# Activation parts side by side, buffers 96 bytes on, and three orders of matmuls in the FFN input

## The chip, the cores and the metric

The kernel runs on one core of a Trainium2 chip. The metric is the device time of one execution in microseconds; less is better. Each kernel is executed several times, and one further execution is taken with the hardware profiler. Distances of two matmuls are given in nanoseconds, from start to start.

## What is computed

A decoder trunk of two layers over 256 positions of width 2048, in float32. Every sub-layer takes an RMS norm of the stream, modulates it by shift, scale and gate, which come from a conditioning vector, and adds its output to the stream. Layer 0 mixes positions by a gated recurrence and by attention with forget gates, layer 1 by gated linear attention. Both layers end with the SwiGLU FFN of width 5632, which is the part that the change touches most:

```python
def swiglu(h, w_in, w_out):
    a, u = jnp.split(h @ w_in, 2, axis=-1)
    return (jax.nn.silu(a) * u) @ w_out
...
        h = modulate(rms_norm(x, norm_ffn_gain[layer]), sh2, sc2)
        x = x + g2[:, None, :] * swiglu(h, ffn_w_in[layer], ffn_w_out[layer])
```

## The kernel before

**Split operands.** Matmuls run on float32r operands, which the engine takes in one pass at less than full precision. Each operand is therefore split into a high part (the value rounded) and a low part (the rest), and a product is hi·hi + hi·lo + lo·hi, summed in PSUM. Weights arrive from DRAM in tiles of 128 x 2048 floats (raw), and for every half of such a tile ACT writes hi (line 166) and DVE lo (line 168). Activations are kept in tiles of eight buffers called h: four blocks of 128 features, each for 256 positions, in both parts. Such a tile is [128, 2, 4, 256] before: all four blocks of the high part first, then all four of the low part. These tiles have the names hT_s, hT_f, hT_n (normed inputs) and ct_m, ct_f (mixer and FFN outputs).

**Two kinds of product.** An ordinary product (lines 192 to 194) has the activations as stationary operand, 128 positions at a time, and 512 columns of weights as moving operand; three matmuls for each block and each half of the positions. One with 16 blocks has 96 matmuls. There are 38 such products (4 acc_A, 8 acc_B, 8 acc_O, 12 acc_C, 2 acc_F, and the start's, acc_s, which amount to 4), and the FFN output, acc_G, has 22 blocks for each of 4 column tiles in each layer. A turned product (lines 204 and 205) is used for the FFN input. There the weights are stationary, and the activations move:

```python
                nc.tensor.matmul(o, hi[:, cs], both, start=(kt == 0), stop=False, skip_group_check=True)
                nc.tensor.matmul(o[:, :T], lo[:, cs], both[:, 0], start=False, stop=(kt == KT - 1), skip_group_check=True)
```

The operand `both` is the high and the low part of one block, 2 x 256 columns, read as two runs that lie 4 KiB apart. So the first of the two matmuls has 512 columns and writes hi·hi into the first and hi·lo into the second half of a PSUM bank; the second has 256 columns and adds lo·hi to the first half. The document calls the two a pair. Every matmul has a weight load of its own, also where two in a row have the same stationary operand.

**FFN.** The 5632 columns are 22 chunks of 256 gate and 256 value columns. Chunk 0 is an ordinary product, chunks 1 to 21 are turned, each in two halves of 32 pairs (16 blocks x 2 column tiles). After a half, `done` copies the second half of the bank (ACT, line 1158), adds the first half (DVE, line 1159), applies silu, multiplies and splits the result into a ct_f tile. The chunks form four groups, (0 to 5), (6 to 11), (12 to 17) and (18 to 21); the FFN output of a group (acc_G, four column tiles) is computed one chunk after the group's last, so it stands after chunks 6, 12, 18 and 21.

**Order.** `drive()` goes through the pieces of all products in one order, keeps weight splits three pieces ahead and loads up to six further, and puts the steps of the recurrences between them. Among these are narrow products (line 290, 128 stationary by 256 moving columns) and the decay exponents ex (line 470), which have 512 moving columns out of the constant lvl.

**Where buffers lie.** Pools are laid out one behind the other. In the built program, silu_c and cols lie at 16512 and 24704 bytes of each partition; ident, lvl, tri, lmask, cmask and st follow from 25792 on and start at multiples of 64. The raw tiles start at 56992, hi at 81568, lo at 97952, h at 114336; all of these, and the buffers behind them, start 32 bytes past a multiple of 64 (160 past a multiple of 256 for raw, hi, lo and h).

Of the kernel before, what the change touches and what calls it, by code (L numbers as in the profile page):

```python
# [7 lines left out]
F32 = mybir.dt.float32  # L8
F32R = mybir.dt.float32r
I32 = mybir.dt.int32  # L10
AF = mybir.ActivationFunctionType
ALU = mybir.AluOpType
# [3 lines left out]
P = 128  # L16
T = 256
D = 2048
KT = D // P
# [3 lines left out]
LEVELS = (64, 32, 16, 8, 4, 2, 1)  # L23
FFN_GROUPS = ((0, 6), (6, 12), (12, 18), (18, 22))
LOOKAHEAD = 2
RAWS = 3
HIS = 4
FIRST = 4
# [19 lines left out]
NCOLS = 270  # L48
# [17 lines left out]
def build(tc, ctx, a, out):  # L66
    nc = tc.nc
    const = ctx.enter_context(tc.tile_pool(name="const", bufs=1))
    small = ctx.enter_context(tc.tile_pool(name="small", bufs=2))
    rawp = ctx.enter_context(tc.tile_pool(name="rawp", bufs=RAWS))  # L70
    piecep = ctx.enter_context(tc.tile_pool(name="piecep", bufs=HIS))
    hpool = ctx.enter_context(tc.tile_pool(name="hpool", bufs=8))
# [3 lines left out]
    def ps_mix(name):  # L76
        return env["pm"].tile([P, 512], F32, tag="pm", name=name)

    def h_tile(name):
        return hpool.tile([P, 2, 4, T], F32R, tag="h", name=name)  # L80


    silu_c = const.tile([P, D], F32, name="silu_c")
    cols = const.tile([P, NCOLS], F32, name="cols")
    ident = const.tile([P, P], F32, name="ident")
    lvl = const.tile([P, 9 * P], F32R, name="lvl")
    tri = const.tile([P, 2 * P], F32R, name="tri")
# [52 lines left out]

    def add(name, w, act, done, before=None, rate=0.0, first=False, last=False, turned=False):
        p = Product(name, w, act, done, before, rate)
        p.first, p.last, p.turned = first, last, turned
        pieces.extend((p, k) for k in range(2 * len(w)))

    urgent = []
# [49 lines left out]
    def multiply_turned(p, k, hi, lo):  # L196

        for kk in range(4):
            kt = k * 4 + kk
            both = p.act(kt)  # L200
            for c in range(2):
                cs = slice(kk * 256 + c * P, kk * 256 + (c + 1) * P)
                o = p.ps[:, c]
                nc.tensor.matmul(o, hi[:, cs], both, start=(kt == 0), stop=False, skip_group_check=True)  # L204
                nc.tensor.matmul(o[:, :T], lo[:, cs], both[:, 0], start=False, stop=(kt == KT - 1), skip_group_check=True)  # L205

    def run_jobs(n):
        while jobs and n > 0:
# [26 lines left out]
    def drive():  # L235
        i = 0
        while i < len(pieces):
# [7 lines left out]
            run_jobs(quota())  # L245
            for m in range(i, i + max(n, LOOKAHEAD + 1)):
                split(m)
            for m in range(i + LOOKAHEAD + 1, min(i + LOOKAHEAD + 7, len(pieces))):
                load(m)
# [19 lines left out]
    def act_of(tiles):  # L269
        def act(kt, t=None):  # L270
            tl = tiles(kt // 4) if callable(tiles) else tiles[kt // 4]
            if t is None:
                return tl[:, :, kt % 4, :]
            sl = t if isinstance(t, slice) else slice(t * P, (t + 1) * P)
            return tl[:, 0, kt % 4, sl], tl[:, 1, kt % 4, sl]
        return act

    def narrow_product(pool, act, w, n, name):
# [68 lines left out]
    def norm_tile(t):  # L347

        acol, bcol, hT, name = env["norm"]
        pool = env["pool"]  # L350
        r = rstd_of(env["ss"], t, f"{name}{t}")
        diag = pool.tile([P, P], F32, tag="diag", name=f"diag_{name}{t}", bufs=1)
        env["diag"] = nc.vector.tensor_scalar(diag, ident, r, None, ALU.mult).ins
        for nb in range(4):
            ps = ps_mix(f"xT_{name}_{nb}_{t}")
            tm = pool.tile([P, 512], F32, tag="hm", name=f"hm_{name}_{nb}_{t}", bufs=2)
            for kk in range(4):
                sl = slice(kk * P, (kk + 1) * P)
                nc.tensor.matmul(ps[:, sl], env["x"][nb][:, t, sl], diag, start=True, stop=True)
            for kk in range(4):  # L360
                kt = nb * 4 + kk
                sl = slice(kk * P, (kk + 1) * P)
                if kk < 2:
                    nc.vector.tensor_scalar(tm[:, sl], ps[:, sl], acol[:, kt:kt + 1], bcol[:, kt:kt + 1], ALU.mult, ALU.add)
                else:
                    nc.scalar.activation(tm[:, sl], ps[:, sl], AF.Identity, bias=bcol[:, kt:kt + 1], scale=acol[:, kt:kt + 1])
            hv = hT[nb][:, 0, :, t * P:(t + 1) * P]
            lv = hT[nb][:, 1, :, t * P:(t + 1) * P]
            src = tm.rearrange("p (k t) -> p k t", k=4)
            nc.scalar.copy(out=hv, in_=src)  # L370
            nc.vector.tensor_tensor(lv, src, hv, ALU.subtract)  # L371
# [9 lines left out]
    def split_columns(src, gains, key, n):  # L381
        c, k0 = ct_pair(key, n)
        if gains is None:
            hv = c[:, 0, k0:k0 + 2].rearrange("p k t -> p (k t)")
            lv = c[:, 1, k0:k0 + 2].rearrange("p k t -> p (k t)")
            nc.scalar.copy(out=hv, in_=src)
            nc.vector.tensor_tensor(lv, src, hv, ALU.subtract)
        else:
            for k in range(2):
                s = src[:, k * T:(k + 1) * T]  # L390
                nc.scalar.activation(c[:, 0, k0 + k], s, AF.Copy, scale=gains[k])
                nc.vector.scalar_tensor_tensor(c[:, 1, k0 + k], s, gains[k], c[:, 0, k0 + k], ALU.mult, ALU.subtract)

    lines = {}

# [555 lines left out]
    def start():  # L951
# [13 lines left out]
        hT, raw_w, raw_m = [], {}, {}  # L965
# [25 lines left out]
        def operand(kt):  # L991
            if kt % 4 == 0:
                hT.append(h_tile(f"hT_s{kt // 4}"))
            h = hT[-1]
            k = slice(kt, kt + 1)
            tm = pool.tile([P, T], F32, tag="tm", name=f"tm_s{kt}")
            nc.scalar.activation(tm, xT[:, kt, :], AF.Identity, bias=modc[0, 0][:, k], scale=acol[:, k])
            nc.scalar.copy(out=h[:, 0, kt % 4], in_=tm)
            nc.vector.tensor_tensor(h[:, 1, kt % 4], tm, h[:, 0, kt % 4], ALU.subtract)

        fetch_columns(0)
        fetch_columns(1)
# [1 line left out]
        with tc.tile_pool(name="ps_t", bufs=4, space=PSUM) as pt:  # L1004
            env["pm"] = pt
            for nb in range(4):
                ps = ps_mix(f"c_{nb}")
                sl = slice(nb * 512, (nb + 1) * 512)
# [13 lines left out]
            for nb in range(4):  # L1022
# [5 lines left out]
                for half in range(2):  # L1028
                    ps = ps_mix(f"xT_{nb}_{half}")
# [4 lines left out]
                    k0 = nb * 4 + half * 2  # L1034
# [11 lines left out]
        for kt in range(KT):  # L1046
# [8 lines left out]
            for n in (1, 3, 0, 2):  # L1055
                hi, lo = ws[n // 2]
                sl = slice((n % 2) * 512, (n % 2 + 1) * 512)
                for t in range(2):
                    a_hi, a_lo = act(kt, t)
                    o = acc[n][t]  # L1060
# [93 lines left out]
    def done_ffn_turned(l, i, half):  # L1154

        def done(ps):
            s = env["pool"].tile([P, 2, T], F32, tag="fs", name=f"fs{l}_{i}_{half}")
            nc.scalar.copy(out=s, in_=ps[:, :, T:])
            nc.vector.tensor_tensor(s, s, ps[:, :, :T], ALU.add)
            if i == FFN_GROUPS[-1][1] - 1 and half == 1:  # L1160
                silu_then_exp_ln(s[:, 0], s[:, 0])
            else:
                nc.scalar.activation(s[:, 0], s[:, 0], AF.Silu)
            nc.vector.tensor_tensor(s[:, 0], s[:, 0], s[:, 1], ALU.mult)
            gi = group_of(i)
            c, k0 = ct_pair(f"f{l}{gi}", i - FFN_GROUPS[gi][0])
            nc.scalar.copy(out=c[:, 0, k0 + half], in_=s[:, 0])
            nc.vector.tensor_tensor(c[:, 1, k0 + half], s[:, 0], c[:, 0, k0 + half], ALU.subtract)
        return done

    def done_ffn(l, i):
# [50 lines left out]
    def quads(w):  # L1222
        return [w[qd] for qd in range(4)]

    def add_ffn(l, rate):
        w1, wt, w2 = a["ffn_w_in"], a["ffn_w_turned"], a["ffn_w_out"]
        n = 0
        for gi, (b, e) in enumerate(FFN_GROUPS):
            while n < min(e + 1, FFN_GROUPS[-1][1]):
                before = {0: lambda: begin_ffn(l), 4: lambda: begin_row(l)}.get(n)  # L1230
                if n == 0:
                    add(f"F{l}_{n}", quads(w1[l]), now_act, done_ffn(l, n), before, rate, True)
                else:
                    for half in range(2):
                        m = 2 * n + half - 2
                        add(f"F{l}_{n}_{half}", [wt[l, m, qd] for qd in range(2)], now_act, done_ffn_turned(l, n, half),
                            before if half == 0 else None, rate, turned=True)
                n += 1
            for nb in range(4):
                add(f"G{l}_{gi}_{nb}", [w2[l, b // 2 + qd, nb] for qd in range((e - b) // 2)], ct_act(f"f{l}{gi}"),  # L1240
                    done_ffn_out(l, gi, nb), rate=rate, last=gi == len(FFN_GROUPS) - 1 and nb == 3)
# [32 lines left out]
    for u in range(4):  # L1274
        for half in range(2):
            before = (lambda: job(fox_gates(), TICKS["fox_gates"])) if (u, half) == (0, 0) else None
# [119 lines left out]
```

## Time and profile before

| | |
|---|---|
| median of 3 runs | 2531.12 us (2529.35 to 2532.55) |
| profiled execution | 2535.65 us |
| its span, first to last instruction | 2533.9 us |
| PE matmul busy | 2469.4 us, 12492 matmuls |
| DVE busy | 1825.2 us |
| ACT busy | 1211.2 us |
| mean granted TensorE clock | 0.996 of 2.4 GHz |

The profile lists each matmul from its start to its modelled end, and successive matmuls overlap. So the busy time of a group says little of its cost; the distance between two starts does, or the number of them in a stretch of known length.

### The profile page before, as it was taken

What the parts mean: (1) busy time and instruction counts of PE and PEld (TensorE: products, weight loads), DVE (VectorE), ACT (ScalarE), POOL (GpSimd) and SP (SyncE); (2) the same over time, 40 slices, a digit from 0 to 9 for tenths busy, and PEclk for the clock granted to TensorE, in tenths of its full rate; (3) what the DMA queues carried; (4) which work ended last, traced back from release to release, by engine and by line L of the source; (5) the groups of instructions that cost most, each with busy time, mean ns of one, the idle gap of its engine ahead of it and who ended that gap; (6) DMA issues with size and microseconds to landing.
All of it is one profiled execution on the core that took longest, in us unless ns stands there. A gap on an engine that the chain in (4) does not pass through costs nothing.

```text
span 2533.9 us, 31800 instructions
## 1 busy us (share of the span) xinstructions
PE 2469.4 (97%) x12492; PEld 2078.0 (82%) x12492; DVE 1825.2 (72%) x2143; ACT 1211.2 (48%) x1768; POOL 89.4 (4%) x174
## 2 busy tenths in 40 slices
PE   5799999999999999999999999999999999999999
PEld 4678887887888888888888888888888888888887
DVE  6977887877788877777777777776686555555555
ACT  4365555545444444444445545554544344344443
POOL 0000000000000000000000000000000000000000
PEclk9999999999999999999999999999999999999999
DMA  9964767885798877777776566667476555555554
GB/s 382 421 262 150 279 255 284 345 314 208 281 358 344 313 275 292 283 272 292 285 274 226 205 243 235 244 254 272 172 299 244 199 183 184 199 183 185 197 183 150
DMA packets 93865, 647.69 MB, mean 256 GB/s; under 512 B 10418, under 2 KB 10994, under 8 KB 16402
## 3 DMA queue, kind: packets, MB, share of 16 engines
q1 hardware_dynamic: 70290, 476.59, 50.4%
q0 software_dynamic: 23424, 169.07, 17.6%
q8 instruction: 98, 1.61, 0.2%
q14 instruction: 53, 0.43, 0.0%
HBM read 641.39 MB, written 4.23 MB: 255 GB/s over the span
## 4 chain that ended last, share of the span: by engine, by line
PE 92%; DVE 6%; ACT 1%; issue 0%; DMA 0%; SPq 0%; ACTq 0%; DVEq 0%
PE acc_F L204 25%; PE acc_F L205 13%; PE acc_G L192 6%; PE acc_G L194 6%; PE acc_G L193 6%; PE acc_C L194 3%; PE acc_C L192 3%; PE acc_C L193 3%; DVE mod_s L108 3%; PE acc_B L192 2%; PE acc_B L194 2%; PE acc_B L193 2%; PE acc_O L192 2%; PE acc_O L193 2%; PE acc_O L194 2%; DVE lo_s L168 1%
## 5 line engine op out<-in xcount | busy, mean ns | idle before, releaser
L204 PE MATMUL acc_F<-hT_f,hi 128*128 128x512 f32 x2688 | 948.1, 398 | 0.0
L205 PE MATMUL acc_F<-hT_f,lo 128*128 128x256 f32 x2688 | 753.9, 280 | 0.0
L168 DVE TENSOR_TENSOR lo<-raw_F,hi 128x1024 fp32r<-128x1024 f32 x352 | 430.0, 1224 | 292.3 <-ACT hi L166 292.0
L166 ACT CAST hi<-raw_F 128x1024 fp32r<-128x1024 f32 x352 | 369.8, 1051 | 498.4 <-PE acc_F L204 281.0
L204 PEld LDWEIGHTS acc_F<-hT_f,hi 128*128 128x128 f32 x2688 | 504.9, 188 | 124.6
L205 PEld LDWEIGHTS acc_F<-hT_f,lo 128*128 128x128 f32 x2688 | 507.4, 189 | 0.6
L108 DVE SCALAR_TENSOR_TENSOR mod<-mod,silu_c 128x2048 f32<-128x2048 f32 x160 | 365.4, 2285 | 1.2 <-DMA mod<-in_mod_w_dram 1.2
L166 ACT CAST hi<-raw_G 128x1024 fp32r<-128x1024 f32 x176 | 185.3, 1054 | 273.2 <-PE acc_G L194 206.7
L168 DVE TENSOR_TENSOR lo<-raw_G,hi 128x1024 fp32r<-128x1024 f32 x176 | 214.3, 1223 | 133.4 <-ACT hi L166 133.3
L192 PE MATMUL acc_G<-hi,ct_f 128*128 128x512 f32 x704 | 273.9, 389 | 1.6 <-DVE res_G L419 1.6
L193 PE MATMUL acc_G<-lo,ct_f 128*128 128x512 f32 x704 | 273.9, 389 | 0.0
L194 PE MATMUL acc_G<-hi,ct_f 128*128 128x512 f32 x704 | 273.7, 389 | 0.0
L168 DVE TENSOR_TENSOR lo<-raw_C,hi 128x1024 fp32r<-128x1024 f32 x96 | 116.7, 1222 | 58.8 <-ACT hi L166 58.4
L192 PEld LDWEIGHTS acc_G<-hi,ct_f 128*128 128x128 f32 x704 | 132.2, 188 | 30.0 <-DVE res_G L419 2.4
L192 PE MATMUL acc_C<-hi,hT_n 128*128 128x512 f32 x384 | 154.3, 402 | 0.9 <-ACT hT_n L370 0.9
L194 PEld LDWEIGHTS acc_G<-hi,ct_f 128*128 128x128 f32 x704 | 132.1, 188 | 27.5
L193 PEld LDWEIGHTS acc_G<-lo,ct_f 128*128 128x128 f32 x704 | 132.2, 188 | 27.1
L194 PE MATMUL acc_C<-hi,hT_n 128*128 128x512 f32 x384 | 150.5, 392 | 0.7 <-DVE hT_n L371 0.7
L193 PE MATMUL acc_C<-lo,hT_n 128*128 128x512 f32 x384 | 150.9, 393 | 0.0
L166 ACT CAST hi<-raw_C 128x1024 fp32r<-128x1024 f32 x96 | 100.7, 1052 | 95.9 <-PE acc_C L194 89.5
L103 POOL DMA_DIRECT2D mod<-in_mod_w_dram x160 | 84.7, 530 | 1683.2 <-DVE mod L108 1542.2
L166 ACT CAST hi<-raw_O 128x1024 fp32r<-128x1024 f32 x64 | 67.4, 1054 | 80.9 <-PE acc_O L194 72.1
(345 smaller groups left out, 3485.8 us busy)
## 6 DMA issues: line engine op xcount, KB each, us to landing
raw_F<-in_ffn_w_turned_dram SPq DMA_DIRECT2D x168, 1024.0 KB, 4.8
mod<-in_mod_w_dram POOLq DMA_DIRECT2D x160, 1024.0 KB, 5.1
raw_G<-in_ffn_w_out_dram SPq DMA_DIRECT2D x88, 1024.0 KB, 4.8
raw_C<-in_gla_w_in_dram SPq DMA_DIRECT2D x48, 1024.0 KB, 5.7
mod_s<-in_mod_w_dram SPq DMA_DIRECT2D x32, 1024.0 KB, 10.8
raw_B<-in_ab_w_in_dram SPq DMA_DIRECT2D x32, 1024.0 KB, 5.6
raw_s<-in_start_w_dram SPq DMA_DIRECT2D x16, 1024.0 KB, 9.4
raw_A<-in_ab_w_in_dram SPq DMA_DIRECT2D x16, 1024.0 KB, 4.8
```

The lines of the kernel that those rows point to most:

```text
L103: nc.gpsimd.dma_start(out=tile, in_=a["mod_w"][l, part * KT + j])
L108: nc.vector.scalar_tensor_tensor(tile, tile, 1.0, silu_c, ALU.mult, ALU.mult, accum_out=modc[l, part][:, j:j + 1])
L166: nc.scalar.copy(out=hi, in_=w)
L168: env["lo"] = nc.vector.tensor_tensor(lo, w, hi, ALU.subtract)
L192: nc.tensor.matmul(o, a_hi, w_hi, start=(kt == 0), stop=False)
L193: nc.tensor.matmul(o, a_hi, w_lo, start=False, stop=False)
L194: nc.tensor.matmul(o, a_lo, w_hi, start=False, stop=(kt == last))
L204: nc.tensor.matmul(o, hi[:, cs], both, start=(kt == 0), stop=False, skip_group_check=True)
L205: nc.tensor.matmul(o[:, :T], lo[:, cs], both[:, 0], start=False, stop=(kt == KT - 1), skip_group_check=True)
```

## The change

Four edits. First, the activation tile is [128, 4, 2, 256]: the two parts of a block lie side by side, and `both` is one run of 512 columns. All writers and readers of these tiles follow. Second, the buffer behind cols is 24 floats longer, so everything behind it lies 96 bytes further on: raw, hi, lo, h and the buffers behind them now start on a multiple of 256 bytes (or of 64 for some smaller ones), and ident, lvl, tri, lmask, cmask and st 32 bytes past a multiple of 64. Third, the turned products take one of three orders by their chunk's number modulo 3: "pairs" (0), as before; "twos" (1), where the two 512-column matmuls of a block come first and then the two of 256; "threes" (2), where the 512-column matmul is split in two of 256 that add to the same half of the bank, so that three matmuls of 256 follow one another. Fourth, `done` of a threes chunk only copies the first half, and has no add.

```diff
-        return hpool.tile([P, 2, 4, T], F32R, tag="h", name=name)
+        return hpool.tile([P, 4, 2, T], F32R, tag="h", name=name)
...
-    cols = const.tile([P, NCOLS], F32, name="cols")
+    cols = const.tile([P, NCOLS + 24], F32, name="cols")[:, :NCOLS]
...
+            def high(c):
+                nc.tensor.matmul(p.ps[:, c], hi[:, col[c]], both, start=(kt == 0), stop=False, skip_group_check=True)
+
+            def low(c):
+                nc.tensor.matmul(p.ps[:, c, :T], lo[:, col[c]], both[:, :T], start=False, stop=(kt == KT - 1), skip_group_check=True)
+
+            if p.order == "pairs":
+                for c in range(2):
+                    high(c)
+                    low(c)
+            elif p.order == "twos":
+                high(0)
+                high(1)
+                low(0)
+                low(1)
+            else:
+                for c in range(2):
+                    o = p.ps[:, c, :T]
+                    nc.tensor.matmul(o, hi[:, col[c]], both[:, :T], start=(kt == 0), stop=False)
+                    nc.tensor.matmul(o, hi[:, col[c]], both[:, T:], start=False, stop=False)
+                    nc.tensor.matmul(o, lo[:, col[c]], both[:, :T], start=False, stop=(kt == KT - 1))
...
-                return tl[:, :, kt % 4, :]
+                return tl[:, kt % 4].rearrange("p s t -> p (s t)")
...
-            nc.scalar.copy(out=s, in_=ps[:, :, T:])
-            nc.vector.tensor_tensor(s, s, ps[:, :, :T], ALU.add)
+            if i % 3 == 2:
+                nc.scalar.copy(out=s, in_=ps[:, :, :T])
+            else:
+                nc.scalar.copy(out=s, in_=ps[:, :, T:])
+                nc.vector.tensor_tensor(s, s, ps[:, :, :T], ALU.add)
...
-                            before if half == 0 else None, rate, turned=True)
+                            before if half == 0 else None, rate, turned=ORDERS[n % 3])
```

On PE, where chunk 1 of layer 0 ends and chunk 2 begins, the order before is (out<-moving,stationary; acc_F_1_1 is the second half of chunk 1, acc_F_2_0 the first of chunk 2):

```order
L204 MATMUL acc_F_1_1_5092<-hT_f_3_4672,hi_5109 128x512
L205 MATMUL acc_F_1_1_5092<-hT_f_3_4672,lo_5110 128x256
L204 MATMUL acc_F_2_0_5187<-hT_f_0_4669,hi_5129 128x512
L205 MATMUL acc_F_2_0_5187<-hT_f_0_4669,lo_5130 128x256
L204 MATMUL acc_F_2_0_5187<-hT_f_0_4669,hi_5129 128x512
```

At the same place of the changed kernel:

```order
L206 MATMUL acc_F_1_1_5092<-hT_f_3_4672,hi_5109 128x512 x2
L209 MATMUL acc_F_1_1_5092<-hT_f_3_4672,lo_5110 128x256 x2
L223 MATMUL acc_F_2_0_5187<-hT_f_0_4669,hi_5129 128x256
L224 MATMUL acc_F_2_0_5187<-hT_f_0_4669,hi_5129 128x256
L225 MATMUL acc_F_2_0_5187<-hT_f_0_4669,lo_5130 128x256
```

Chunk 1 now has its 512-column matmuls two by two, and chunk 2 has none of 512 columns.

On DVE, around the end of the first half of chunk 2, before (mod is the conditioning's sum, line 108):

```order
L168 TENSOR_TENSOR lo_5301<-raw_F_2_1_1_5133,hi_5300 128x1024
L1159 TENSOR_TENSOR fs_2_0_5269<-fs_2_0_5269,acc_F_2_0_5187 128x512
L168 TENSOR_TENSOR lo_5321<-raw_F_3_0_0_5185,hi_5320 128x1024
L1164 TENSOR_TENSOR fs_2_0_5269<-fs_2_0_5269 128x256
L168 TENSOR_TENSOR lo_5343<-raw_F_3_0_0_5185,hi_5342 128x1024
```

and after:

```order
L170 TENSOR_TENSOR lo_5340<-raw_F_2_1_1_5133,hi_5339 128x1024
L1187 TENSOR_TENSOR fs_2_0_5301<-fs_2_0_5301 128x256
L170 TENSOR_TENSOR lo_5368<-raw_F_3_0_0_5185,hi_5367 128x1024
L1191 TENSOR_TENSOR ct_f_1_5305<-fs_2_0_5301,ct_f_1_5305 128x256
L170 TENSOR_TENSOR lo_5398<-raw_F_3_0_0_5185,hi_5397 128x1024
```

The add out of PSUM (line 1159) is gone there, and the rest of DVE's work stands as before.

## Rows read from the trace of the kernel before

**Rows 1.** The page, busy time, share of the span and instructions by engine:

```profile
PE 2469.4 (97%) x12492; PEld 2078.0 (82%) x12492; DVE 1825.2 (72%) x2143; ACT 1211.2 (48%) x1768; POOL 89.4 (4%) x174
```

**Rows 2.** The page, shares of the chain that ended last, by engine:

```profile
PE 92%; DVE 6%; ACT 1%; issue 0%; DMA 0%; SPq 0%; ACTq 0%; DVEq 0%
```

**Rows 3.** Groups of matmuls: names, shapes, count, busy us, mean ns, idle before:

```profile
L204 PE MATMUL acc_F<-hT_f,hi 128*128 128x512 f32 x2688 | 948.1, 398 | 0.0
L205 PE MATMUL acc_F<-hT_f,lo 128*128 128x256 f32 x2688 | 753.9, 280 | 0.0
...
L193 PE MATMUL acc_G<-lo,ct_f 128*128 128x512 f32 x704 | 273.9, 389 | 0.0
```

**Rows 4.** Stretch, acc_G alone: us, PE busy, clock, DMA share, GB/s:

```profile
1180.00:1220.00 40.00, 40.00 (x178) 1.00 0.82 305
```

**Rows 5.** Stretches, line 204: us, PE busy, PEld busy, clock, DMA share, GB/s:

```profile
850.00:950.00 100.00, 100.00 (x284) 53.18 (x283) 1.00 0.75 280
1820.00:1920.00 100.00, 99.76 (x288) 54.00 (x288) 1.00 0.76 293
```

**Rows 6.** Timeline of PE, acc_G into acc_F: start us, duration us, instruction:

```profile
838.74 0.39 PE L193 MATMUL acc_G<-lo,ct_f 128*128 128x512 f32 x1
838.97 0.39 PE L194 MATMUL acc_G<-hi,ct_f 128*128 128x512 f32 x1
839.20 0.39 PE L204 MATMUL acc_F<-hT_f,hi 128*128 128x512 f32 x1
839.42 0.28 PE L205 MATMUL acc_F<-hT_f,lo 128*128 128x256 f32 x1
839.53 0.40 PE L204 MATMUL acc_F<-hT_f,hi 128*128 128x512 f32 x1
839.77 0.28 PE L205 MATMUL acc_F<-hT_f,lo 128*128 128x256 f32 x1
839.88 0.40 PE L204 MATMUL acc_F<-hT_f,hi 128*128 128x512 f32 x1
840.13 0.28 PE L205 MATMUL acc_F<-hT_f,lo 128*128 128x256 f32 x1
840.25 0.40 PE L204 MATMUL acc_F<-hT_f,hi 128*128 128x512 f32 x1
```

**Rows 7.** Timeline of PE, the narrow product of layer 1 and what follows:

```profile
1386.75 3.95 PE L290 MATMUL nacc_glow<-hT_n,nw_glow 128*128 128x256 f32 x32
1390.53 0.40 PE L194 MATMUL acc_C<-hi,hT_n 128*128 128x512 f32 x1
```

**Rows 8.** Timeline of PE, the narrow product of layer 0, first stretch:

```profile
329.85 2.49 PE L290 MATMUL nacc_fb<-hT_s,nw_fb 128*128 128x256 f32 x19
332.17 0.27 PE L654 MATMUL oT_A<-ident,o_A 128*128 128x128 f32 x1
```

**Rows 9.** Chain that ended last: start us, us, what; 128-column matmuls:

```profile
617.94 3.57 PE xT_f L359 x32
```

**Rows 10.** Groups of DVE, columns as in Rows 3, with the releaser:

```profile
L168 DVE TENSOR_TENSOR lo<-raw_F,hi 128x1024 fp32r<-128x1024 f32 x352 | 430.0, 1224 | 292.3 <-ACT hi L166 292.0
...
L1159 DVE TENSOR_TENSOR fs<-fs,acc_F 128x512 f32<-128x512 f32 x84 | 57.2, 681 | 0.6 <-ACT fs L1158 0.6
```

**Rows 11.** Timeline of PE, four ex matmuls amid acc_C in layer 1:

```profile
1408.44 0.39 PE L193 MATMUL acc_C<-lo,hT_n 128*128 128x512 f32 x1
1408.67 1.10 PE L470 MATMUL ex_C<-lvl,lf_C 128*128 128x512 f32 x4
1409.60 0.40 PE L194 MATMUL acc_C<-hi,hT_n 128*128 128x512 f32 x1
...
1411.45 0.39 PE L193 MATMUL acc_C<-lo,hT_n 128*128 128x512 f32 x1
```

**Rows 12.** Start: PE, PEld, DVE, ACT, POOL busy, clock, DMA share, GB/s:

```profile
60.00:80.00 20.00, 15.65 (x66) 12.34 (x67) 20.00 (x26) 8.73 (x12) 0.00 (x0) 1.00 1.01 423
80.00:100.00 20.00, 15.51 (x66) 11.82 (x65) 20.00 (x26) 8.72 (x12) 0.00 (x0) 1.00 1.01 420
```

More of the change, by code (lines that the diff above doesn't have):

```diff
@@ L25 @@
 LOOKAHEAD = 2
+ORDERS = ("pairs", "twos", "threes")
 RAWS = 3
@@ L142, in add @@
         p = Product(name, w, act, done, before, rate)
-        p.first, p.last, p.turned = first, last, turned
+        p.first, p.last, p.turned = first, last, bool(turned)
+        p.order = turned
         pieces.extend((p, k) for k in range(2 * len(w)))
@@ L200, in multiply_turned @@
             both = p.act(kt)
[L201 to L205, printed above, removed]
+            col = [slice(kk * 256 + c * P, kk * 256 + (c + 1) * P) for c in range(2)]
+            def high(c):
[17 more added lines that the diff above has]
+                    nc.tensor.matmul(o, lo[:, col[c]], both[:, :T], start=False, stop=(kt == KT - 1))
     def run_jobs(n):
@@ L272, in act @@
             if t is None:
-                return tl[:, :, kt % 4, :]
+                return tl[:, kt % 4].rearrange("p s t -> p (s t)")
             sl = t if isinstance(t, slice) else slice(t * P, (t + 1) * P)
-            return tl[:, 0, kt % 4, sl], tl[:, 1, kt % 4, sl]
+            return tl[:, kt % 4, 0, sl], tl[:, kt % 4, 1, sl]
         return act
@@ L366, in norm_tile @@
                     nc.scalar.activation(tm[:, sl], ps[:, sl], AF.Identity, bias=bcol[:, kt:kt + 1], scale=acol[:, kt:kt + 1])
-            hv = hT[nb][:, 0, :, t * P:(t + 1) * P]
-            lv = hT[nb][:, 1, :, t * P:(t + 1) * P]
+            hv = hT[nb][:, :, 0, t * P:(t + 1) * P]
+            lv = hT[nb][:, :, 1, t * P:(t + 1) * P]
             src = tm.rearrange("p (k t) -> p k t", k=4)
@@ L383, in split_columns @@
         if gains is None:
-            hv = c[:, 0, k0:k0 + 2].rearrange("p k t -> p (k t)")
-            lv = c[:, 1, k0:k0 + 2].rearrange("p k t -> p (k t)")
+            hv, lv = c[:, k0:k0 + 2, 0], c[:, k0:k0 + 2, 1]
+            src = src.rearrange("p (k t) -> p k t", k=2)
             nc.scalar.copy(out=hv, in_=src)
@@ L390, in split_columns @@
                 s = src[:, k * T:(k + 1) * T]
-                nc.scalar.activation(c[:, 0, k0 + k], s, AF.Copy, scale=gains[k])
-                nc.vector.scalar_tensor_tensor(c[:, 1, k0 + k], s, gains[k], c[:, 0, k0 + k], ALU.mult, ALU.subtract)
+                nc.scalar.activation(c[:, k0 + k, 0], s, AF.Copy, scale=gains[k])
+                nc.vector.scalar_tensor_tensor(c[:, k0 + k, 1], s, gains[k], c[:, k0 + k, 0], ALU.mult, ALU.subtract)
     lines = {}
@@ L997, in operand @@
             nc.scalar.activation(tm, xT[:, kt, :], AF.Identity, bias=modc[0, 0][:, k], scale=acol[:, k])
-            nc.scalar.copy(out=h[:, 0, kt % 4], in_=tm)
-            nc.vector.tensor_tensor(h[:, 1, kt % 4], tm, h[:, 0, kt % 4], ALU.subtract)
+            nc.scalar.copy(out=h[:, kt % 4, 0], in_=tm)
+            nc.vector.tensor_tensor(h[:, kt % 4, 1], tm, h[:, kt % 4, 0], ALU.subtract)
         fetch_columns(0)
@@ L1166, in done @@
             c, k0 = ct_pair(f"f{l}{gi}", i - FFN_GROUPS[gi][0])
-            nc.scalar.copy(out=c[:, 0, k0 + half], in_=s[:, 0])
-            nc.vector.tensor_tensor(c[:, 1, k0 + half], s[:, 0], c[:, 0, k0 + half], ALU.subtract)
+            nc.scalar.copy(out=c[:, k0 + half, 0], in_=s[:, 0])
+            nc.vector.tensor_tensor(c[:, k0 + half, 1], s[:, 0], c[:, k0 + half, 0], ALU.subtract)
         return done
```

## The prediction

> **What bounds the kernel now.** I read the busy times first, then the chain that ended last, then the stretches of the FFN. PE is busy 97% of the span and holds 92% of the chain [rows 1, 2], so time goes only where matmuls start further apart or closer together. A busy time can't tell that: matmuls overlap, a listed one lasts 389 or 398 ns [rows 3] while the next starts some 230 ns later [rows 6]. What counts is start to start.
>
> Three such distances carry the rest. **512 columns after 512 columns** (acc_G): 178 matmuls fall into 40 us, the first of them begun up to 0.39 us before [rows 4], so 40.39 / 178 = 226.9 ns; 512 columns at 2.4 GHz, the level granted there, are 213.3, so 13.6 ns lie on top. **A pair of the FFN input** (512 columns with hi, then 256 with lo): in 100 us stretches the trace counts 283 and 288 weight loads of line 204 [rows 5], so 353.4 ns per pair in one and 347.2 in the other; four more such stretches between 660 and 2330 us count like the first. The same code has two paces. The starts show how the slower one comes about [rows 6]: coming from acc_G at its steady 0.23, the first 512 also takes 0.22 to 0.23 us, and its operand lies in two runs. The two runs cost nothing there. The next 256 takes 0.11, and from then on the 512s take 0.24, 0.25, 0.23, repeating every three pairs. So the pace depends on what the engine's pipeline was doing before, not on the address pattern alone. **256 after 256** (the narrow product): 32 in 1390.53 - 1386.75 = 3.78 us, 118.1 ns each [rows 7]; in the other narrow product, with transposes close by, 19 in 2.32 us, 122 ns [rows 8]. The floor for any matmul with a weight load of its own is shown by the 128-column ones: 3.57 / 32 = 111.6 ns [rows 9].
>
> All 2688 pairs [rows 3] are changed: 21 chunks x 2 halves x 32 pairs x 2 layers. The order goes by chunk number modulo 3, which gives 896 pairs to each order.
>
> **The change part by part.**
>
> *Chunks 2, 5, ... ("threes"): 256, 256, 256 in place of 512, 256.* One more matmul and weight load per pair. 3 x 118.1 = 354.3 against 353.4: +0.9 ns x 896 = +0.8 us. Ends: at the floor 3 x 111.6 = 334.8, -16.7 us; at 122, 366, +11.3 us. I take 118.1, the long undisturbed run with the same operand width.
>
> *Chunks 1, 4, ... ("twos"): 512, 512, 256, 256.* Every group of acc_G products is followed by such a chunk, so it starts from the steady state. Its best is 2 x 226.9 + 2 x 118.1 = 690.0, 345.0 per pair, -8.4 x 896 = -7.5 us; with floors for the 256s 338.5, -13.4 us; at the pace of today's pairs 0. The trace has no such sequence; since a 512 that follows a 256 takes 0.23 to 0.25 [rows 6], I take half of the first gain, -3.8 us.
>
> *Chunks 3, 6, ... ("pairs"): order as before, operand in one run of 512.* The operand itself gains nothing, by the first 512 after acc_G [rows 6]. But these chunks no longer begin from acc_G; they come after a threes chunk. After interruptions the trace has both paces (the stretch at 1820 is the quick one [rows 5]). Ends 0 and -6.2 x 896 = -5.6 us; I take the middle, -2.8.
>
> *Buffers 96 bytes on.* Before, every buffer after cols starts 32 bytes past a 64-byte step or, for the small constants, on one; after, it is the other way round. For DVE and ACT I cost it at nothing: while PE is 97% busy they wait (DVE's lo idles 292 us for hi [rows 10]). For matmuls the nearest rows are the ex matmuls, whose moving operand lvl starts on a 64-byte step: 4 in 1409.60 - 1408.67 = 0.93 us, 232 ns, and from their start 12 matmuls take 2.78 us where 12 x 0.2269 is 2.72 [rows 11]. Moving and weight operand differ in phase there, and after the change they agree again, as they do before in acc_G. So I take 0, with both ends as rivals below.
>
> The rows say that a different phase is felt. The Trainium skill says otherwise: "SBUF — State Buffer", Specifications, has 16-byte cachelines that want two hits each, and 96 is six of them, so by that rule the shift is worth exactly 0 and both alignment rivals fall away. The ex rows speak against so simple a rule, though lvl differs in more than its phase.
>
> *In the start,* DVE is busy 20.00 of 20 us while the DMA engines are full too [rows 12]; the mod_s and lo work of DVE isn't touched, so quicker or slower landing by a few per cent hides behind it: 0, and 1 to 3 us lost if landing became slower.
>
> *Off the path.* 28 adds of DVE go, 681 ns each [rows 10], 19 us of an engine that waits; 0. The ACT copies stay, one PSUM source moves to the other half. Writes of activation parts get a wider stride between runs; nobody waits for them long. No wait and no DMA is added, and two neighbouring loads on SP change places in two spots.
>
> **Sum:** +0.8 - 3.8 - 2.8 = -5.8 us, ends about -36 and +11. The profiled execution took 2535.65 us with a span of 2533.9; it gives 2530. The median of the three runs is 2531.12, 4.5 lower, and I carry the difference over to it: **2525**. Within this case 2512 to 2536.
>
> **Rivals.**
>
> *A: the start on a 256-byte step takes part of the 13.6 ns away.* Every large buffer starts off a 64-byte step today, every 512-column matmul shows the excess, so a common cause is possible. There are 7552 of them after the change: 1792 in twos and pairs, 2112 in acc_G (3 x 704 [rows 3]) and 38 x 96 = 3648 in the other products. Half the excess is 6.8 x 7552 = 51 us, 2480; all of it 103 us, 2428. Against it: the ex matmuls, aligned in their moving operand, were slower and not quicker.
>
> The Trainium skill, "TensorE: Matmul & The Clock Gate", "Wait — 56ns, not 53.3ns?", gives N / 2.4 + 2.5 ns at full clock. By it 512 columns would take 215.8, and if the phase is what keeps this kernel from it, an estimate from that page is 11.1 x 7552 = 84 us, 2447. The rows are 11 ns above the page's figure, and no row says why.
>
> *B: slower. A moving operand on a 64-byte step is the costly one.* This is what the ex matmuls show if read plainly: 232 against 226.9, right out of a steady run [rows 11]. 5.1 x 7552 = +39 us, 2564 with the gains above; the place is every product, not the FFN alone. It decides from (5.8 + 5) / 7552 = 1.4 ns per 512-column matmul on. Against it: only four stand in a row there, among matmuls of the other phase, and the ones behind them are slow as well.
>
> *C: nothing changes.* Twos and pairs both fall into the 353 ns rhythm and threes run at 118: 2532. For it: acc_G led into that rhythm at once. This lies inside my first case, as does its bad end, threes at 122 ns: 2540.
>
> **How the numbers follow.** 0.2% is 5 us, about what a measurement here can tell from no change. No effect of the address: 0.55, and since -5.8 is just over the bound I split it 0.30 faster, 0.22 same (C), 0.03 slower (threes at 122). A: 0.27, nearly all faster (0.26 and 0.01 same). B: 0.18, as 0.14 slower, 0.03 same, 0.01 faster. That gives 0.57, 0.26, 0.17. The likeliest is 2525. The range has to take in most of A and a part of B: 2440 leaves out A's far end (0.06), 2556 leaves out most of B (0.11), 0.03 for the unforeseen.
>
> **What would show it.** Weight loads of the FFN lines in 100 us: threes 847 (118.1 ns), pairs 283 to 288, twos 283 to 290 of each kind. acc_G start to start: 227 if the address does nothing, 220 or less for A, 230 or more for B; since acc_G's order is untouched, it judges the shift alone. The ex matmuls, off the step after the change, would tell B from a mere difference of phase. I am wrong in the step on threes if 256 after 256 isn't 118 in a long run, and in the step on the address if acc_G moves.

## The result and the profile after

The changed kernel takes 2536.31 us (median of 15 runs, 2535.13 to 2537.82), the kernel before, run beside it, 2531.33 (2529.35 to 2536.25). The ratio is 1.0019, with a 95% interval of 1.0011 to 1.0027: slower by 5.0 us (2.8 to 6.8). The forecast was 2525, faster by 6. So the sign was wrong, and what happened is about the smallest change that can be told from none.

The two profiled executions hide this: 2535.34 us after, 2535.65 before. The profile of before was 4.3 us above its median, that of after 1.0 below. Part of this is the granted clock ahead of the FFN, 0.98 against 1.00 of 2.4 GHz from 200 to 300 us; by the first turned product the profile of after is 2.4 us ahead, at 635.51 us against 637.93. The windows view, first of before, then of after (us, PE busy, matmuls, granted clock, DMA share, GB/s):

```profile
200.00:300.00 100.00, 97.68 (x514) 0.98 0.56 204
```

```profile
200.00:300.00 100.00, 97.68 (x521) 1.00 0.59 212
```

So what the change did is read from distances of starts, as in the prediction, inside the FFN, where the clock is 1.00 in both.

The page of the profile of after, against [rows 1 and 3]:

```profile
PE 2469.5 (97%) x13388; PEld 2122.2 (84%) x13388; DVE 1808.8 (71%) x2115; ACT 1215.1 (48%) x1768; POOL 89.8 (4%) x174
...
L206 PE MATMUL acc_F<-hT_f,hi 128*128 128x512 f32 x1792 | 598.2, 397 | 0.0
...
L223 PE MATMUL acc_F<-hT_f,hi 128*128 128x256 f32 x896 | 253.5, 283 | 0.0
```

There are 896 more matmuls in the same busy time, and DVE works 16 us less, at no gain in time: it was an engine that waits.

Each order's price can be read from whole chunks. The timeline of PE in after, layer 0, where one chunk ends and the next begins (start us, length us, then line, tiles and shape; chunk 8 is threes, 9 pairs, 10 twos, 11 threes again):

```profile
859.28 0.28 PE L223 MATMUL acc_F<-hT_f,hi 128*128 128x256 f32 x1
...
882.31 0.40 PE L206 MATMUL acc_F<-hT_f,hi 128*128 128x512 f32 x1
...
904.92 0.64 PE L206 MATMUL acc_F<-hT_f,hi 128*128 128x512 f32 x2
...
927.23 0.28 PE L223 MATMUL acc_F<-hT_f,hi 128*128 128x256 f32 x1
...
950.27 0.40 PE L206 MATMUL acc_F<-hT_f,hi 128*128 128x512 f32 x1
```

A chunk has two halves of 32 pairs, 64 in all. Chunk 8 lasts 882.31 - 859.28 = 23.03 us, which is 359.8 ns in place of a pair; chunk 9 22.61, 353.3; chunk 10 22.31, 348.6; chunk 11 23.04, 360.0. The other chunks read alike (threes 359.8 to 361.1, twos 348.2 to 349.7, pairs 353.3), but for one chunk of pairs that is interrupted, at 350.3, which it was in the kernel before too. The means over all chunks of an order are 360.0, 348.6 and 353.1. Over all its 2688 pairs the kernel before has 352.6 (353.3 nearly everywhere, 346.7 for some 117 us, as in the second of [rows 5]). Threes therefore cost 896 x 7.4 = 6.6 us, twos give 896 x 4.0 = 3.6, pairs cost 896 x 0.5 = 0.4: **+3.4 us**, of the 5.0 measured; the interval of the measurement takes in the rest. All 2688 taken together agree: 353.9 ns after against 352.6 before is 3.5 us.

Inside the threes hardly anything varies: the next matmul starts 0.12 us after the last (116 to 121 ns, and 120 in nearly all).

```profile
861.07 0.28 PE L223 MATMUL acc_F<-hT_f,hi 128*128 128x256 f32 x1
861.19 0.28 PE L224 MATMUL acc_F<-hT_f,hi 128*128 128x256 f32 x1
861.31 0.28 PE L225 MATMUL acc_F<-hT_f,lo 128*128 128x256 f32 x1
```

In the twos (below, chunk 10), two 512s take 0.46 us and two 256s 0.23, so a set of four, worth two pairs, 0.69, in other sets 0.70:

```profile
905.64 0.63 PE L206 MATMUL acc_F<-hT_f,hi 128*128 128x512 f32 x2
906.10 0.40 PE L209 MATMUL acc_F<-hT_f,lo 128*128 128x256 f32 x2
906.33 0.63 PE L206 MATMUL acc_F<-hT_f,hi 128*128 128x512 f32 x2
```

What the order leaves alone did not move, though every operand lies 96 bytes further on. acc_G in the same 40 us as [rows 4], from the windows view (busy, matmuls, clock, DMA share, GB/s), has 179 matmuls against 178:

```profile
1180.00:1220.00 40.00, 40.00 (x179) 1.00 0.81 301
```

The narrow product of layer 1 [rows 7] and the ex matmuls [rows 11] in the timeline of after:

```profile
1385.24 3.95 PE L310 MATMUL nacc_glow<-hT_n,nw_glow 128*128 128x256 f32 x32
1389.03 0.40 PE L196 MATMUL acc_C<-hi,hT_n 128*128 128x512 f32 x1
...
1407.17 1.10 PE L490 MATMUL ex_C<-lvl,lf_C 128*128 128x512 f32 x4
1408.10 0.40 PE L196 MATMUL acc_C<-hi,hT_n 128*128 128x512 f32 x1
```

3.79 / 32 = 118.4 ns, 118.1 before; 0.93 us for four, as before, although lvl has left the 64-byte step. Its partner lf_C moved by the same 96 bytes, so the distance between the two is what it was.

Two questions stood open. Is it the order alone? And why does a matmul of 256 columns take 118 in one place and 120 in another?

### The profile page after: what moved, and what is told of

Same layout as the page of the kernel before. It is cut to its first block, busy times and chain, and to the rows that moved or that the text cites. A ratio compares the mean times of both kernels' runs of the same rounds, so it can differ in the third digit from the quotient of the medians.

```text
span 2533.6 us, 33484 instructions
## 1 busy us (share of the span) xinstructions
PE 2469.5 (97%) x13388; PEld 2122.2 (84%) x13388; DVE 1808.8 (71%) x2115; ACT 1215.1 (48%) x1768; POOL 89.8 (4%) x174
## 4 chain that ended last, share of the span: by engine, by line
PE 92%; DVE 6%; ACT 1%; issue 0%; DMA 0%; ACTq 0%; POOLq 0%
PE acc_F L206 17%; PE acc_F L209 8%; PE acc_G L194 6%; PE acc_G L196 6%; PE acc_G L195 6%; PE acc_F L224 4%; PE acc_F L225 4%; PE acc_F L223 4%; PE acc_C L196 3%; PE acc_C L194 3%; PE acc_C L195 3%; DVE mod_s L109 3%; PE acc_B L194 2%; PE acc_B L196 2%; PE acc_B L195 2%; PE acc_O L194 2%
## 5 line engine op out<-in xcount | busy, mean ns | idle before, releaser
L168 ACT CAST hi<-raw_F 128x1024 fp32r<-128x1024 f32 x352 | 370.0, 1052 | 500.2 <-PE acc_F L206 233.3
L206 PE MATMUL acc_F<-hT_f,hi 128*128 128x512 f32 x1792 | 598.2, 397 | 0.0
L209 PE MATMUL acc_F<-hT_f,lo 128*128 128x256 f32 x1792 | 427.7, 279 | 0.0
L206 PEld LDWEIGHTS acc_F<-hT_f,hi 128*128 128x128 f32 x1792 | 305.4, 188 | 42.0
L225 PE MATMUL acc_F<-hT_f,lo 128*128 128x256 f32 x896 | 253.6, 283 | 0.0
L224 PE MATMUL acc_F<-hT_f,hi 128*128 128x256 f32 x896 | 253.5, 283 | 0.0
L223 PE MATMUL acc_F<-hT_f,hi 128*128 128x256 f32 x896 | 253.5, 283 | 0.0
L224 PEld LDWEIGHTS acc_F<-hT_f,hi 128*128 128x128 f32 x896 | 172.0, 192 | 0.0
L223 PEld LDWEIGHTS acc_F<-hT_f,hi 128*128 128x128 f32 x896 | 171.9, 192 | 0.0
L194 PE MATMUL acc_C<-hi,hT_n 128*128 128x512 f32 x384 | 154.3, 402 | 0.9 <-ACT hT_n L390 0.9
```

The source lines that it names most:

```text
L168: nc.scalar.copy(out=hi, in_=w)
L194: nc.tensor.matmul(o, a_hi, w_hi, start=(kt == 0), stop=False)
L206: nc.tensor.matmul(p.ps[:, c], hi[:, col[c]], both, start=(kt == 0), stop=False, skip_group_check=True)
L209: nc.tensor.matmul(p.ps[:, c, :T], lo[:, col[c]], both[:, :T], start=False, stop=(kt == KT - 1), skip_group_check=True)
L223: nc.tensor.matmul(o, hi[:, col[c]], both[:, :T], start=(kt == 0), stop=False)
L224: nc.tensor.matmul(o, hi[:, col[c]], both[:, T:], start=False, stop=False)
```

## One order at a time

Three kernels keep the layout and the shift of the changed kernel and differ in the table of orders, with the add in `done` where an order needs it:

```diff
-ORDERS = ("pairs", "twos", "threes")
+ORDERS = ("pairs", "pairs", "pairs")     # all_pairs
+ORDERS = ("twos", "twos", "twos")        # all_twos
+ORDERS = ("threes", "threes", "threes")  # all_threes
...
-            if i % 3 == 2:
+            if ORDERS[i % 3] == "threes":
```

**all_pairs**

> The changed kernel with every turned chunk in the order of before (512, 256): what the layout and the 96 bytes do alone. If only the order of the matmul lengths sets the pace (theory: rhythm): 353.3 ns per pair, acc_G at 226.9, and within 0.1% of before, about 2531 to 2533. If the layout or the shift cost something outside the matmuls (rival): part of the 5 us that the changed kernel lost is here, 2533 to 2536. If the operand in one run or the new start helps pairs: 347 ns per pair and about 2518.

Measured: 2533.82 us against 2533.27 for the kernel before, ratio 1.0002 (0.9994 to 1.0011). Weight loads of the 512s in two stretches (windows view: us, PEld busy, loads, granted clock, DMA share, GB/s):

```profile
850.00:950.00 100.00, 53.18 (x284) 1.00 0.75 278
1820.00:1910.00 90.00, 48.75 (x260) 1.00 0.79 302
```

100 us / 284 is a pace of 353 as in the first of [rows 5], 90 / 260 is 346, the quick one. So side by side and 96 bytes on are together worth nothing that can be told (-0.06% to +0.11%), and the quick stretch at 1820 us comes at the same place of the program as before, with two runs or with one.

**all_twos**

> The changed kernel with every turned chunk in the order 512, 512, 256, 256. Rhythm: 348.5 ns per pair as in the twos chunks of the changed kernel, so 2688 x (348.5 - 352.6) = -11 us, about 2520. If the twos chunks were quick only because they followed the settled acc_G or stood beside chunks of another order: 353 in the chunks that follow one of the same order, and 2528 to 2532.

Measured: 2521.45 us, ratio 0.9950 (0.9937 to 0.9962). Weight loads of the 512s:

```profile
850.00:950.00 100.00, 43.74 (x288) 1.00 0.77 284
```

From start to start the pairs take 348.3 nearly everywhere and 348.4 on the mean; 2688 x (352.6 - 348.4) = 11.3 us, and the ratio says 12.7. It beats both kernels.

**all_threes**

> The changed kernel with every turned chunk as three matmuls of 256. Rhythm: 360 ns in place of a pair, so 2688 x (360.0 - 352.6) = +20 us, about 2551. If a long run settles to the pace of the narrow product (118.1 each, 354.3): +5 us, 2536.

Measured: 2553.73 us, ratio 1.0085 (1.0070 to 1.0101). All weight loads of the turned products:

```profile
850.00:950.00 100.00, 100.00 (x835) 1.00 0.78 282
```

100 us / 835 = 119.8 ns. 2688 x 7.4 = 19.9 us is what the distances give, the ratio says 21.5. The saved adds on DVE show nowhere in the time. A third of twos' gain and a third of threes' loss, -4 and +7, make the greater part of what the change did.

**before_twos** has nothing of the change but the order of twos: the kernel before, with two runs 4 KiB apart and the old addresses.

```diff
+            cols_ = [slice(kk * 256 + c * P, kk * 256 + (c + 1) * P) for c in range(2)]
             for c in range(2):
-                cs = slice(kk * 256 + c * P, kk * 256 + (c + 1) * P)
-                o = p.ps[:, c]
-                nc.tensor.matmul(o, hi[:, cs], both, start=(kt == 0), stop=False, skip_group_check=True)
-                nc.tensor.matmul(o[:, :T], lo[:, cs], both[:, 0], start=False, stop=(kt == KT - 1), skip_group_check=True)
+                nc.tensor.matmul(p.ps[:, c], hi[:, cols_[c]], both, start=(kt == 0), stop=False, skip_group_check=True)
+            for c in range(2):
+                nc.tensor.matmul(p.ps[:, c, :T], lo[:, cols_[c]], both[:, 0], start=False, stop=(kt == KT - 1), skip_group_check=True)
```

> The kernel before with the order 512, 512, 256, 256 in all turned chunks and nothing else: operand in two runs, buffers where they were. If the order alone makes the gain (rhythm): 348.3 ns per pair and the time of all_twos, about 2521. If the operand in one run or the 96 bytes are needed for it: 353 ns and 2531 to 2533.

Measured: 2522.11 us, ratio 0.9956 (0.9943 to 0.9969). The timeline of PE reads like that of twos above:

```profile
905.02 0.63 PE L203 MATMUL acc_F<-hT_f,hi 128*128 128x512 f32 x2
905.49 0.39 PE L205 MATMUL acc_F<-hT_f,lo 128*128 128x256 f32 x2
905.72 0.62 PE L203 MATMUL acc_F<-hT_f,hi 128*128 128x512 f32 x2
```

The order alone makes the gain, one run or two.

## The price of one matmul by itself

**probe** puts blocks of matmuls behind the last product of the kernel before, with nothing else at work. Each follows 24 matmuls of 512 columns that settle the engine (line 1315), has one weight load per matmul, and adds to one PSUM tile. Weights and moving operand come from one hi and one h buffer. Two of the blocks:

```diff
+        # 256, weights 512 bytes apart, one operand
+        settle()
+        for q in range(96):
+            nc.tensor.matmul(pr[:, 0, :T], ws(q), half(0), start=False, stop=False, skip_group_check=True)
+        # 512, operand 32 bytes on
+        settle()
+        for q in range(48):
+            nc.tensor.matmul(pr[:, 0], ws(q), mv[:, 8 + (q % 3) * 512:520 + (q % 3) * 512], start=False, stop=False, skip_group_check=True)
```

> The kernel before, with about 2000 matmuls added behind its last product, in fifteen blocks, each behind 24 matmuls of 512 columns that settle the pace; the sums go nowhere, and the time is about 300 us longer for that. Rhythm: pairs 353 with the operand in one run and in two; twos 348.5; threes 360; 256 after 256 at 120 for any weights; 512s that start 32 bytes on, or come from lvl, settle to 227 as all others. Rival (addresses): 256 after 256 at 118 where weights lie 128 bytes apart or are used twice, as in the narrow product, and 120 where they lie 512 apart; 512s that start on a 64-byte step stay at 231 to 236. Longer groups than two (four, eight, sixteen of each length) go below 348.5 if a change of length is what costs, and not if the pace of 256 after 256 is.

The timeline merges equal neighbours, so a block's length is its own start to that of the settling matmuls behind it. Below are 256s with eight weight slices 512 bytes apart (line 1374), then 512s with the operand 32 bytes on (1378), 512s that read lvl (1382) and 512s of which every second opens its sum anew (1386):

```profile
2718.26 11.68 PE L1374 MATMUL probe_ps<-probe_m,probe_w 128*128 128x256 f32 x96
2729.77 0.40 PE L1315 MATMUL probe_ps<-probe_w,probe_m 128*128 128x512 f32 x1
...
2735.24 11.37 PE L1378 MATMUL probe_ps<-probe_m,probe_w 128*128 128x512 f32 x48
2746.44 0.86 PE L1315 MATMUL probe_ps<-probe_w,probe_m 128*128 128x512 f32 x3
...
2751.91 11.37 PE L1382 MATMUL probe_ps<-lvl,probe_w 128*128 128x512 f32 x48
2763.12 5.64 PE L1315 MATMUL probe_ps<-probe_w,probe_m 128*128 128x512 f32 x24
2768.59 11.04 PE L1386 MATMUL probe_ps<-probe_m,probe_w 128*128 128x512 f32 x48
2779.47 0.39 PE L1315 MATMUL probe_ps<-probe_w,probe_m 128*128 128x512 f32 x1
```

That is 11.51 / 96 = 119.9 ns for the 256s (the same with one weight slice for all), 233.3 for the 512s 32 bytes on, 233.5 from lvl, and 226.7 for the last. The threes block takes 120.0, the pairs 353.3 with one run and with two, the twos 348.3, orders of four, eight and sixteen at a time 350.8, 349.2 and 347.3 per pair (the sixteens have only three rounds). These repeat from the second or third round on. Fours cost more than twos, so it is not simply each change of length that costs. 256s whose weight slices lie 128 bytes apart, each used twice as in the narrow product, take 117.5. Pairs that follow eight matmuls of 128 columns, or two of 256, still fall into 353. So a 256 has no one price, and neither has a 512: addresses do count, and not the way the change moved them.

**phase** asks which distance it is: the same blocks with the moving operand offset against the weights, both in buffers that start alike modulo 256 bytes.

> The kernel before with matmuls added behind its last product, as in the probe: the start of the moving operand against the start of the weights, modulo 512 bytes, in steps from 16 to 448 bytes. In the probe 512 columns took 226.7 ns at equal phase and 233.3 with the operand 32 bytes on; 256 took 120.0 at equal phase and 117.5 where the weights went on by 128 bytes. If the phase between the two sets the pace (theory): some offsets of 64 bytes and more stay at 226.7 or go below, offsets that are no multiple of 64 sit at 233.3, and 256s at one fixed offset of 128, 256 or 384 bytes sit below 120. If only being off a 64-byte step counts (rival): all multiples of 64 give 226.7 and 120, and 117.5 comes from the weights' moving on alone, which the last block shows with one matmul for each weight slice.

The timeline of PE, 512s with the operand 16, 192 and 256 bytes on, then 256s with 32 and 128, and last 256s whose weights move on by 128 bytes each time; each block is followed by settling matmuls:

```profile
2532.55 11.28 PE L1321 MATMUL probe_ps<-probe_m,probe_w 128*128 128x512 f32 x48
2543.67 5.63 PE L1315 MATMUL probe_ps<-probe_w,probe_m 128*128 128x512 f32 x24
...
2598.97 11.36 PE L1337 MATMUL probe_ps<-probe_m,probe_w 128*128 128x512 f32 x48
2610.17 5.62 PE L1315 MATMUL probe_ps<-probe_w,probe_m 128*128 128x512 f32 x24
2615.63 11.04 PE L1341 MATMUL probe_ps<-probe_m,probe_w 128*128 128x512 f32 x48
2626.51 5.60 PE L1315 MATMUL probe_ps<-probe_w,probe_m 128*128 128x512 f32 x24
...
2665.26 7.63 PE L1353 MATMUL probe_ps<-probe_m,probe_w 128*128 128x256 f32 x64
2672.72 5.63 PE L1315 MATMUL probe_ps<-probe_w,probe_m 128*128 128x512 f32 x24
2678.19 7.84 PE L1357 MATMUL probe_ps<-probe_m,probe_w 128*128 128x256 f32 x64
2685.86 5.63 PE L1315 MATMUL probe_ps<-probe_w,probe_m 128*128 128x512 f32 x24
...
2825.90 7.73 PE L1403 MATMUL probe_ps<-probe_m,probe_w 128*128 128x256 f32 x64
2833.47 0.86 PE L1315 MATMUL probe_ps<-probe_w,probe_m 128*128 128x512 f32 x3
```

By these rows 231.7, 233.3, 226.7, 116.6, 119.8 and 118.3 ns with the blocks' beginnings. The steady distances, from the starts of each block's second half (probe gave those that phase has no block for):

| operand against weights | 0 | 16 | 32 | 64 | 96 | 128 | 192 | 256 | 384 | 448 |
|---|---|---|---|---|---|---|---|---|---|---|
| 512 after 512, ns | 226.7 | 231.7 | 233.3 | 228.9 | 233.3 | 233.3 | 233.3 | 226.7 | 233.3 | 233.3 |
| 256 after 256, ns | 120.0 | | 116.7 | | | 120.0 | | 120.0 | 120.0 | |
| a pair, ns | 353.3 | | 346.7 | | | 351.1 | | 353.3 | 351.1 | |
| a pair in twos, ns | 348.3 | | | | | 348.2 | | 348.4 | | |

256 bytes on is like 0 in every row of the table. At a fixed offset the pace goes by the difference of the two starts, and not in one direction: 32 bytes make a 512 dearer by 6.6 and a 256 cheaper by 3.3 ns. Neither expectation held whole. For 512s the rival falls, since 64 and 128 bytes give 228.9 and 233.3; but of the larger offsets only 256 stays at 226.7, and 16 gives 231.7 and not 233.3, which the theory did not say. For 256s the theory was wrong: fixed offsets of 128 and 384 take 120.0, as 0 does. Yet the last block, whose weights go through just these offsets, takes 118.3, near the narrow product's 118.1, as the rival had it. So the offset of a matmul is not the whole: it also counts that the weights move on from one to the next.

**pad32** takes this into the real kernel: 32 bytes between the lo and the h buffers of the kernel before, so that activations and weights differ by 32 in every product.

```diff
+    padp = ctx.enter_context(tc.tile_pool(name="padp", bufs=1))
+    gap = padp.tile([P, 8], F32, name="gap")
+    nc.vector.memset(gap, 0.0)
     hpool = ctx.enter_context(tc.tile_pool(name="hpool", bufs=8))
```

> The kernel before with 32 bytes of nothing between the buffers of lo and those called h, so that in every product the activations start 32 bytes past the weights' phase, in whichever of the two roles they are. No other edit. Theory that the difference of the two starts sets the pace (from the blocks of the run phase): the 512s of ordinary products, acc_G among them, go from 226.7 to 233.3 ns, 5760 x 6.6 = +38 us; the pairs of the FFN input go from 353.3 to 346.7 where they are not there already (some 2390 of 2688), -15.8 us; in all +22 us, about 2553. Rival that only where a buffer itself starts counts, or nothing of that kind in the real kernel, where buffers are written while they are read: h now starts on a multiple of 64, which the change's shift also gave it at no gain, so 2531 within 3 us, acc_G at 226.9 and pairs at 353.3.

Measured: 2545.71 us against 2534.11, ratio 1.0047 (1.0031 to 1.0064), +11.6 us. The windows view of acc_G's matmuls, then of the pairs' 512 weight loads in both layers:

```profile
1180.00:1220.00 40.00, 40.00 (x173) 1.00 0.76 289
```

```profile
850.00:950.00 100.00, 54.09 (x289) 1.00 0.79 296
1830.00:1930.00 100.00, 53.91 (x288) 1.00 0.77 294
```

acc_G has 173 matmuls where [rows 4] has 178: 40.39 / 173 = 233.5 ns. The pairs take 346.7 to 347.0 nearly everywhere, 288 or 289 per 100 us, also right behind acc_G, where [rows 6] shows how the kernel before falls into its slow rhythm:

```profile
844.15 0.40 PE L197 MATMUL acc_G<-hi,ct_f 128*128 128x512 f32 x1
844.38 0.40 PE L207 MATMUL acc_F<-hT_f,hi 128*128 128x512 f32 x1
844.62 0.28 PE L208 MATMUL acc_F<-hT_f,lo 128*128 128x256 f32 x1
844.74 0.40 PE L207 MATMUL acc_F<-hT_f,hi 128*128 128x512 f32 x1
844.97 0.28 PE L208 MATMUL acc_F<-hT_f,lo 128*128 128x256 f32 x1
```

So the distance between the operands acts in the real kernel too, with both signs in one kernel, while the same kernel moved as a whole (all_pairs) does not change. In the ordinary products the activations are the stationary operand, so the moving one starts 32 bytes earlier there, an offset that no block had. The sum was too high, +22 for +11.6. From the starts, the pairs gave 15.3 us (15.8 expected) and acc_G cost 2112 x 6.5 = 13.7. But in the other products, which the recurrences interrupt, a 512 went up by some 4 to 5 ns and not by 6.6, so that they cost about 15 us and not 24; that the interruptions are the reason is not shown.

## Why the prediction was wrong

**Threes: the step that failed.** It took 118.1 ns for a 256 that follows a 256 and predicted 847 weight loads in 100 us; all_threes has 835, at 120.0 ns from start to start, and the term is +6.6 us instead of +0.8. With this term alone put right the forecast gain is gone (6.6 - 3.8 - 2.8 = 0.0); the pairs' term does the rest. The row was sound and the width was the same, but its weight slices were not: those of the narrow product lie 128 bytes apart (64 in the other one), those of the FFN 512 bytes apart, at one fixed offset to the operand. Measured apart, the first kind takes 117.5 (each slice twice) or 118.3 (once) and the second 120.0. The doubt was priced, in the end at 122, yet as a bad end of a likely case and not as the value; its time of 2540 should be 2542 by the prediction's own terms (2531 + 11.3, with no gain elsewhere). The "floor" of 111.6 for the other end was read from float32 matmuls, while those of the FFN are float32r, where the least steady 256 was 116.7.

**Twos: right.** -3.8 us forecast, -3.6 measured (896 x 4.0). Half of the way from the present pace to the sum of its parts came out, where the sum of the parts would be 345.0 and 348.6 was measured. That it was half is luck: the half was a choice between two ends, not read from a row, and one of the parts, the 256 at 118.1, was wrong.

**Pairs: wrong by 3.2 us.** The prediction took the middle between two paces, -2.8 us, because these chunks begin behind another kind of matmul. They took 353.3 in every chunk but one, and the chunk that had the quick pace before, chunk 3 of layer 1, lost it. The middle of two states is not a likely value when one of them is what the engine falls into: behind acc_G, behind threes, behind eight matmuls of 128 and behind two of 256 it was 353 each time. What leads into the quick one was not found. The stretch at 1820 us is there in all_pairs, probe and phase too, so it comes with the program; a short one of 14 us at 760 is in the profile of before but not in these three, although probe and phase run the same instructions up to there.

**The 96 bytes: the value 0 was right, its reason half.** acc_G judges it, as the prediction said: 179 and 178 matmuls, where rival A wanted 220 ns or less and rival B 230 or more. A falls, since no offset in the table brings a 512 below 226.7. B falls as it was put: ex, off the step, still takes 232, while acc_G, now on one, stays at 227. The prediction had the better reading in half a sentence, that ex is slow because its two operands differ in phase; it then kept 0.45 for the two rivals that overlook it. If its "after the change they agree again" meant the operands of ex, that was wrong: both lie behind cols, both moved by 96 bytes, and ex kept its 0.93 us.

The Trainium skill, "SBUF — State Buffer", Specifications, has cachelines of 16 bytes, from which the prediction derived that a shift by a multiple of 16 is worth nothing. For both operands together the trace agrees. For one alone it does not: offsets of 16, 64 and 128 bytes, all multiples of 16, give 231.7, 228.9 and 233.3 against 226.7.

By the Trainium skill, "TensorE: Matmul & The Clock Gate", "Wait — 56ns, not 53.3ns?", N / 2.4 + 2.5 gives, as an estimate, 109.2 for a 256. No run here shows that: the least steady distance was 116.7, with a weight load for each matmul.

**Off the path** the prediction held: 16 us less DVE work and no time for it, as all_threes shows with three times as many adds gone.

**The sum.** By the prediction's terms +0.8 - 3.8 - 2.8 = -5.8; by the chunks +6.6 - 3.6 + 0.4 = +3.4. The two wrong terms are 5.8 and 3.2 us off, each small beside a pair's 353 ns (2% and 1%); but 896 of each add up, and the forecast was made of such differences.

## What to carry over

Where an engine runs without a gap, price a reordering by whole sequences that run in the same operands, not by the sum of rows for single instructions: the same shape took 116.7, 118.3 or 120.0 ns by where its weights lay against its moving operand and how they moved on. When the place of an operand is in question, move that operand alone; moving all of them together, as here, gained nothing and left the distance between them untested. And put equal lengths next to each other before adding instructions: 512, 512, 256, 256 in place of 512, 256, 512, 256 gave 0.5% of the kernel by the exchange of two lines, in either layout.

## What was not expected of the hardware

The time from one matmul's start to the next depends on the difference of the start addresses of moving operand and weights, alike at 0 and 256 bytes, and the best offset found is another one for 512 columns (0: 226.7 ns, most others 233.3) than for 256 (32: 116.7, at the others tried 120.0). Where the weights move on by 128 bytes each time, a 256 takes 118.3, though each of the offsets that it passes through costs 120.0 alone. Mixed lengths have a rhythm of their own: at equal phase a pair takes 353.3 although a 512 and a 256 alone sum to 226.7 + 120.0 = 346.7, and the loss is smaller where like lengths are grouped, but not in step with the size of the group (348.3 by twos, 350.8 by fours, 349.2 by eights, 347.3 by sixteens). At 32 bytes it is the other way round: 233.3 + 116.7 = 350.0 alone, 346.7 as a pair. Why is open; the runs show the numbers, not the mechanism. Not tried is a kernel with offset 0 for its ordinary products and 32 for the FFN input alone.
